# Two two-layer transformer models on one core: x in two feature halves, square roots on ScalarE, a held bank, and sums moved ahead

## The chip, the cores and the metric

One core of one Trainium2 chip runs the whole kernel in one launch. The metric is the time of the launch in device microseconds (us), the median of several runs.

## What is computed

One sequence of 512 tokens with 1024 features passes through two models in a row, each with two layers, all in float32. A layer of the first model projects x with `w_in`, runs four groups of attention (softmax with a forget gate; latent attention "mla"; stick breaking; a sliding window with sinks), normalises each group, multiplies by `w_o`, adds 1.414 x and applies a layer norm (ln1), then a gated MLP with a second layer norm (ln2). Cut to what matters here:

```python
for l in range(DEPTH):
    h = x @ w_in[l]
    (..., cq, ckv, kr, ..., wq, wk, wv) = jnp.split(h, points, axis=-1)
    out_b = _mla(cq, ckv, kr, ...)          # rms norms of cq and ckv, then products
    ...
    x = _layernorm(ALPHA * x + y, ln1_g[l], ln1_b[l])
    f = (silu(x @ w_gate[l]) * (x @ w_up[l])) @ w_down[l]
    x = _layernorm(ALPHA * x + f, ln2_g[l], ln2_b[l])
```

A layer of the second model has an MLP, a mixer (differential attention of 4 heads, a short convolution, a linear recurrence) and another MLP, each behind an rms norm; a last rms norm gives the output.

## The kernel before, in words

x is kept transposed in SBUF: 8 tiles X of 128 features by 512 tokens, with its two-part split XH (rounded to fp32r) and XL (the rest). A weight chunk is loaded by SP (`raw`, 3 buffers, L176), cast to `whi` by ScalarE (L181) and subtracted to `wlo` by VectorE (L186), four buffers each. A product is three matmuls, hi by hi, lo by hi and hi by lo (`mm3`, L196 to L198), on 512 tokens, or on half of them (256) where `half_units` and `halves` do one token half after the other, so that one half's vector work lies beside the other's products.

PE's order is written by hand: the order of the program. Work that needs an answer from another engine is put in a list of due times (`later`, a time in us) and each product counts its own time off (`tick`: 0.648 for 512 tokens, 0.327 for 256); what is due is issued between two products. `flush` issues all that is left. Products sum in eight PSUM banks: four of `mm`, which `in_turn` hands out in rotation, passing over banks in `held`; two of `sc`; `pt` and `pv`. In layer2's attention two of the four go over to `sc` (`more_scores`). VectorE's and ScalarE's orders come from a planner, by priority, except where `manual_schedule` keeps the order of the program: at the start of the first layer, and from `w_o`'s last products to the first MLP unit (ln1).

**Start (layer1, l = 0).** Tiles 0 and 1 of x (128 tokens by 1024 features each) are loaded whole, 0 by ScalarE's queue and 1 by SP's (L249); `wake` runs 11 products of zeros (L257); `turn_x` transposes 16 blocks (L266) into four banks, and its `parts` split them to XH and XL (L273, L274). Four chunks of `w_in` (two 128-feature rows each) follow on SP; each is cast in four pieces into the weights of two units, `chq` (L808, L809) and `chm` (L813 to L817). `half_units` then runs both units on the first token half (bank name `hg`). After 4.0 us of counted products `second_half` transposes tiles 2 and 3.

**lat_norm.** Squares of the latent values, sums by PE (`st`), `ve` (L853), then `rsqrt` on VectorE: a first guess by a shift and three Newton steps, 11 small operations (L222 to L228). `bc` (due at 5.2 and 5.9) transposes the result into a bank (L233) and the latent values are scaled.

**wkv and the latent products.** `wkv_evac` empties its bank by four copies, ScalarE and VectorE in turn (L987, L988). Then `g_mla_w` makes four latent values (`mv`, L950), each in a bank of `mm`, and `g_mla_qk(0)` takes two more (`uq`, `uk`).

**ln1 (Norm1 with pace).** `bank` adds a finished bank to X (L422), squares it (L424) and lets GpSimd add it to SA (L426). `half` adds the squares to SQ (L434), due at 3.6, or 5.6 for the second half, sums SA and SQ by PE (L333), finds mean and 1/sigma, and 3.8 later `bc` broadcasts them (L233). `tile_` normalises a tile (L459 to L464). In the first half the eight tiles are spread over the products of the second, and what is left is flushed at the end of them, ahead of `half`.

**layer2's head 0.** Ten counted us after a head's attention, `fn` transposes its 512 by 128 result into `pt` (L1644) and `split_scaled` reads it (L212, L213). Beside the steps of attention a `Fill` runs units of 16 products (`u`) from the two banks of `mm`.

**final_tail.** The last down product runs in two token halves. `consume` adds the bank to X, squares (L1390), applies the gain (L1374), transposes features 0 to 3 (L1378, `fin`); `stats` sums SQ and the squares (L1399), makes `ve` (L1401) and `rsqrt`, transposes features 4 to 7 and scales to the output (L1408, L1409, L1411).

Of the kernel before, what the change touches and what calls it, by code (L numbers as in the profile page):

```python
# [10 lines left out]
F32 = mybir.dt.float32  # L11
# [7 lines left out]
P = 128  # L19
S = 512  # L20
D = 1024
# [58 lines left out]
def model_kernel(ctx: ExitStack, tc: tile.TileContext, A: dict, out: bass.AP, n1=DEPTH, n2=DEPTH):  # L80
# [23 lines left out]
    last = [0]  # L104
# [125 lines left out]

    def bcast(dst, col):

        T.transpose(dst, col.to_broadcast([P, P]), ident)  # L233
# [14 lines left out]
    def load_x(xin, j):  # L248
        (nc.scalar if j in (0, 2) else nc.sync).dma_start(xin[j], A["x"][0, j * P:(j + 1) * P, :])  # L249

    def wake():
# [4 lines left out]
        for i in range(11):  # L256
            T.matmul(ps, z[:, :P], z, start=True, stop=True)  # L257

    def turn_x(xin, hh):
        hs = slice(hh * HALF, (hh + 1) * HALF)  # L260
        xps = []
        for t in range(0, ND, 2):
            ps = (mmt("xT") if t < 4 else sct("xT")).rearrange("p (m s) -> p m s", m=2)
            for m in range(2):
                for b in range(2):
                    T.transpose(ps[:, m, b * P:(b + 1) * P],  # L266
                                xin[2 * hh + b][:, (t + m) * P:(t + m + 1) * P], ident)
            xps.append((t, ps))
# [13 lines left out]
        parts.copies = copies  # L282
# [83 lines left out]
    class Norm1:  # L366
# [50 lines left out]
        def bank(self, hh, t0, bank):  # L417
# [9 lines left out]
            self.sqs.append(s)  # L427

        def half(self, hh, banks):
# [5 lines left out]
            self.sqs = []  # L435

            def stats():
# [48 lines left out]
                later(3.8, bc)  # L486
            later(5.6 if self.pace and hh else 3.6, stats)
# [88 lines left out]
    def g_chunks(ch, evac, ncol=256, bank=mmt):  # L576
        for m in range(ncol // P):
# [3 lines left out]
            for k in range(ND):  # L581
                wh, wl = ch[k // 4]
                mm3(ps, wh[:, k % 4, c], wl[:, k % 4, c], XH[:, k], XL[:, k], k == 0, k == ND - 1, MF)
                if k == ND - 1:
                    let_go("unit")
                    evac(m, ps)
# [158 lines left out]
    def layer1(l):  # L745
        w_in = A["w_in"][l]
        with tc.tile_pool(name="at1", bufs=1) as ap_:
# [39 lines left out]
            chq, chm = [], []  # L787
            if l == 0:
                splits = turn_x(xin, 0)
# [5 lines left out]
            for k0 in range(0, ND, 2):  # L795
                rf = wchunk(w_in, k0 * P, 2, 768, 420, split=False)
                if l == 0 and k0 == 2:
                    load_x(xin, 2)
                if l == 0 and k0 == 4:
                    load_x(xin, 3)  # L800
                if l == 0 and k0 < 4:
                    splits(2)
                if k0 % 4 == 0:
                    chq.append(wsplit(4, 256))
                    chm.append(wsplit(4, 256))
                ks = slice(k0 % 4, k0 % 4 + 2)
                hi, lo = [t[:, ks] for t in chq[-1]]
                SC.copy(hi, rf[:, :, 4:260])  # L808
                V.tensor_sub(lo, rf[:, :, 4:260], hi.bitcast(F32))  # L809
                hi, lo = [t[:, ks] for t in chm[-1]]  # L810
# [7 lines left out]
                if l == 0 and k0 == 4:  # L818
                    splits.copies()
            if l == 0:  # L820
# [3 lines left out]
                later(4.0, second_half)  # L824
# [15 lines left out]
            def lat_norm():  # L840
# [6 lines left out]
                def stats():  # L847
# [18 lines left out]
                    later(5.2, lambda: bc((2,), 0))  # L866
                    later(5.9, lambda: bc((0, 1), NB))
# [116 lines left out]
            def wkv_evac(m, ps):  # L984
                if m == 0:
                    for kv in range(2):
# [221 lines left out]
            drain(gw)  # L1208
            drain(g_mla_qk(0))
# [140 lines left out]
    def layer2(l):  # L1350
# [19 lines left out]
        def final_tail(down, nkt, hview):  # L1370
# [10 lines left out]

            def consume(hh, banks):
# [9 lines left out]
                got = {(j, 0): turn(sct("fin"), j, 0) for j in js}  # L1392

                def stats():
                    st = pvt("st")
                    for a, j in enumerate(js):
                        for i, src in enumerate((SQ[:, j * P:(j + 1) * P], s[:, 0, a * P:(a + 1) * P],
                                                 s[:, 1, a * P:(a + 1) * P])):
                            T.matmul(st[:, a:a + 1], src, mcol, start=(i == 0), stop=(i == 2))  # L1399
# [383 lines left out]
```

## Time and profile before

| | |
|---|---|
| runs | 3172.09 us median of 3 (3172.02 to 3172.25) |
| profiled execution | 3171.67 us, its span 3169.9 us |
| TensorE busy | 3136.2 us, 99% of the span |
| weight loads, VectorE, ScalarE, GpSimd | 84%, 51%, 37%, 4% |
| granted TensorE clock, mean | 0.998 |

Times in the rows count from the start of the span. PE is TensorE, DVE VectorE, ACT ScalarE, POOL GpSimd; SPq and ACTq are the queues that issue transfers. A row of a timeline gives start, duration, engine, line, operation, what it writes and reads, how many follow each other, and in brackets how long the engine sat idle before it and what ended that. Matmuls overlap, so the duration of one is longer than its distance to the next.

### The profile page before, as it was taken

Reading aid. Unit: us, or ns where it says so; the run is one execution under the profiler, and the core shown is the slowest. Engines: PE = TensorE matmul, PEld = TensorE weight load, DVE = VectorE, ACT = ScalarE, POOL = GpSimd, SP = SyncE. Lnnn points to the kernel's source line nnn. Section 1 sums busy time; section 2 is a strip of 40 time slices with the busy share of each in tenths; the row PEclk is TensorE's granted clock in tenths of the full one; section 3 lists DMA queues with packets and bytes.
Section 4 is the critical chain, followed back from the end, with each engine's and each line's share of the span. In section 5 each row is a group of like instructions: output and inputs, shape, how many; then the busy total and the mean of one; then the engine's idle time right before and its main releaser. Section 6 shows DMA issues by size and latency. Waiting matters only on the chain.

```text
span 3169.9 us, 40582 instructions
## 1 busy us (share of the span) xinstructions
PE 3136.2 (99%) x16387; PEld 2651.4 (84%) x16387; DVE 1602.9 (51%) x2849; ACT 1164.8 (37%) x1989; POOL 127.6 (4%) x168
## 2 busy tenths in 40 slices
PE   8999999999999999999999999999999999999999
PEld 7889888988888889988888888888888888788888
DVE  6566333575763334844336764443544336754433
ACT  5454322264543222523223543232323224443322
POOL 1002000020020000000000000000000000000000
PEclk9999999999999999999999999999999999999999
DMA  4121333341203333433333223333333332133322
GB/s 144 44 68 54 97 94 97 115 124 40 78 28 107 100 95 110 123 100 93 98 98 97 71 81 100 100 93 100 95 99 93 97 108 88 57 100 100 93 95 85
DMA packets 283822, 289.97 MB, mean 91 GB/s; under 512 B 10261, under 2 KB 280161, under 8 KB 283633
## 3 DMA queue, kind: packets, MB, share of 16 engines
q1 hardware_dynamic: 280752, 282.73, 29.7%
q0 software_dynamic: 2304, 3.07, 0.5%
q8 instruction: 128, 2.10, 0.3%
q10 hardware_dynamic: 576, 1.57, 0.1%
q14 instruction: 62, 0.50, 0.0%
HBM read 285.22 MB, written 2.11 MB: 91 GB/s over the span
## 4 chain that ended last, share of the span: by engine, by line
PE 92%; DVE 4%; ACT 2%; issue 1%; POOL 1%; DMA 0%; DVEq 0%; ACTq 0%; POOLq 0%; SPq 0%
PE u L196 18%; PE u L197 17%; PE u L198 17%; PE o L196 7%; PE o L197 7%; PE o L198 7%; PE pv L724 2%; PE oh L196 2%; PE oh L197 2%; PE oh L198 2%; PE pt L717 1%; PE ut L598 1%; PE ut L600 1%; PE ut L599 1%; PE sc L1053 1%; PE hg L197 1%
## 5 line engine op out<-in xcount | busy, mean ns | idle before, releaser
L186 DVE TENSOR_TENSOR wlo<-raw,whi 128x1024 fp32r<-128x1024 f32 (+2 forms) x562 | 635.7, 1136 | 847.8 <-ACT whi L181 847.1
L196 PE MATMUL u<-XH,whi 128*128 128x512 f32 x2496 | 980.1, 393 | 0.0
L198 PE MATMUL u<-XH,wlo 128*128 128x512 f32 x2496 | 972.3, 390 | 0.0
L197 PE MATMUL u<-XL,whi 128*128 128x512 f32 x2496 | 971.7, 389 | 0.0
L181 ACT CAST whi<-raw 128x1024 fp32r<-128x1024 f32 (+1 forms) x526 | 540.4, 1028 | 945.0 <-PE o L197 407.8
L198 PEld LDWEIGHTS u<-XH,wlo 128*128 128x128 f32 x2496 | 468.6, 188 | 98.8
L196 PEld LDWEIGHTS u<-XH,whi 128*128 128x128 f32 x2496 | 468.9, 188 | 97.5 <-issue 2.2
L197 PEld LDWEIGHTS u<-XL,whi 128*128 128x128 f32 x2496 | 469.0, 188 | 93.8
L196 PE MATMUL o<-hh,whi 128*128 128x512 f32 x836 | 325.6, 389 | 0.0
L198 PE MATMUL o<-hh,wlo 128*128 128x512 f32 x836 | 325.3, 389 | 0.0
L197 PE MATMUL o<-hl,whi 128*128 128x512 f32 x836 | 325.2, 389 | 0.0
L656 ACT ACTIVATE gs<-gs 128x512 f32<-128x512 f32 x88 | 55.5, 632 | 407.4 <-DVE gs L654 407.2
L198 PEld LDWEIGHTS o<-hh,wlo 128*128 128x128 f32 x836 | 156.9, 188 | 32.6
L197 PEld LDWEIGHTS o<-hl,whi 128*128 128x128 f32 x836 | 157.0, 188 | 32.6
L196 PEld LDWEIGHTS o<-hh,whi 128*128 128x128 f32 x836 | 157.0, 188 | 32.3
L655 DVE TENSOR_TENSOR us<-u,SA 128x512 f32<-128x512 f32 x86 | 59.5, 692 | 165.5 <-PE u L198 165.5
L196 PE MATMUL oh<-hh,whi 128*128 128x256 f32 x440 | 125.0, 284 | 0.0
L198 PE MATMUL oh<-hh,wlo 128*128 128x256 f32 x440 | 124.5, 283 | 0.0
L197 PE MATMUL oh<-hl,whi 128*128 128x256 f32 x440 | 124.5, 283 | 0.0
L654 DVE TENSOR_TENSOR gs<-u,SA 128x512 f32<-128x512 f32 x86 | 58.9, 685 | 89.2 <-PE u L198 89.2
L197 PEld LDWEIGHTS oh<-hl,whi 128*128 128x128 f32 x440 | 84.4, 192 | 0.1
L196 PEld LDWEIGHTS oh<-hh,whi 128*128 128x128 f32 x440 | 84.4, 192 | 0.1
(401 smaller groups left out, 3883.6 us busy)
## 6 DMA issues: line engine op xcount, KB each, us to landing
raw<-ffn_gate SPq DMA_DIRECT2D x88, 512.0 KB, 3.7
raw<-ffn_up SPq DMA_DIRECT2D x88, 512.0 KB, 3.7
raw<-ffn_down SPq DMA_DIRECT2D x82, 512.0 KB, 3.4
raw<-w_in SPq DMA_DIRECT2D x76, 512.0 KB, 3.8
raw<-w_down SPq DMA_DIRECT2D x54, 512.0 KB, 3.4
raw<-w_gate SPq DMA_DIRECT2D x44, 512.0 KB, 3.7
raw<-w_up SPq DMA_DIRECT2D x44, 512.0 KB, 3.7
raw<-w_o SPq DMA_DIRECT2D x16, 512.0 KB, 3.5
```

Of the source, the lines that this page charges most:

```text
L181: SC.copy(hv, rv)
L186: V.tensor_sub(lv[:, ks], rv[:, ks], hv[:, ks].bitcast(F32))
L196: T.matmul(ps, wh, xh, start=start, stop=False)
L197: T.matmul(ps, wh, xl, start=False, stop=False)
L198: T.matmul(ps, wl, xh, start=False, stop=stop)
L598: T.matmul(ps, XH[:, k, js], wh[:, k % 4], start=(k == 0), stop=False)
L599: T.matmul(ps, XH[:, k, js], wl[:, k % 4], start=False, stop=False)
L600: T.matmul(ps, XL[:, k, js], wh[:, k % 4], start=False, stop=(k == ND - 1))
L654: V.tensor_mul(v(gs), v(g), bcv)
L655: V.tensor_mul(v(us), v(u), bcv)
L656: SC.activation(gs, gs, AF.Silu)
L724: T.matmul(self.pv_out(), self.pts[:, a * P:(a + 1) * P], self.vfn(j), start=(a == 0), stop=(a == len(self.kb) - 1))
```

## The change

x's first two tiles arrive in two pieces of 512 features; wake-up is 8 products. Chunk 0 of the weights is asked for behind the first pieces, and only features 0 to 511 are turned ahead of the first products; features 512 to 1023, chunks 4 and 6 and the second token half come at 2.4, 4.4 and 6.4 us of counted products. The four weight buffers are taken as chq, chq, chm, chm in both layers. `lat_norm` and `final_tail` use ScalarE's Sqrt, VectorE's reciprocal and one Newton step. ln1's squares are added between tiles, and its due times change. The wkv bank is held until the four latent values are made. Head 0's result goes to a bank of `mm`. In `final_tail` the transposes and SQ's sums of the second token half move among its products. Cut to its core:

```diff
+    def between(n, fn):
+        n = min(n, len(pend))
+        pend.insert(n, [pend[n - 1][0] if n else 0.0, fn])
+    def rsqrt_by_root(ve, n):
+        y = sp.tile([P, 8], F32, tag="ry", name="ry")[:, :n]
+        q = sp.tile([P, 8], F32, tag="rq", name="rq")[:, :n]
+        SC.activation(q, ve, AF.Sqrt)
+        V.reciprocal(y, q)
+        V.scalar_tensor_tensor(q, y, -0.5, ve, op0=ALU.mult, op1=ALU.mult)
+        V.tensor_mul(q, q, y)
+        V.scalar_tensor_tensor(y, q, 1.5, y, op0=ALU.add, op1=ALU.mult)
+        return y
-        for i in range(11):
+        for i in range(8):
             T.matmul(ps, z[:, :P], z, start=True, stop=True)
...
@@ Norm1.bank, Norm1.half @@
             self.sqs.append(s)
+            if self.pace and hh:
+                between(3 if len(self.sqs) == 2 else 2, lambda: self.add_squares(hh))
...
-                later(3.8, bc)
-            later(5.6 if self.pace and hh else 3.6, stats)
+                later(4.0 if self.pace and hh else 3.8, bc)
+            later(4.2 if self.pace and hh else 3.6, stats)
...
@@ layer1, start @@
-                load_x(xin, 0)
-                load_x(xin, 1)
+                for j in range(2):
+                    load_x(xin, j, 0, D // 2)
                 wake()
+            chq = [wsplit(4, 256) for _ in range(2)]
+            chm = [wsplit(4, 256) for _ in range(2)]
...
+                fetch(0)
+                for j in range(2):
+                    load_x(xin, j, D // 2, D // 2)
+                fetch(2)
+                splits = turn_x(xin, 0, ND // 2)
+                splits(1)
+                weights(0, lambda: splits(1))
+                def stage2():
+                    load_x(xin, 2)
+                    fetch(4)
+                    load_x(xin, 3)
+                    weights(2)
+                    splits.turn(range(ND // 2, ND, 2))
+                    splits(2)
+                    fetch(6)
+                def stage4():
+                    weights(4)
                     splits.copies()
+                    weights(6)
-                later(4.0, second_half)
+                later(2.4, stage2)
+                later(4.4, stage4)
+                later(6.4, second_half)
...
@@ lat_norm @@
-                        r = rsqrt(ve, 2 * NB)
+                        r = rsqrt_by_root(ve, 2 * NB)
-                    later(5.2, lambda: bc((2,), 0))
-                    later(5.9, lambda: bc((0, 1), NB))
+                    later(5.6, lambda: bc((2,), 0))
+                    later(6.3, lambda: bc((0, 1), NB))
...
@@ wkv_evac (m == 0), and behind the latent values @@
+                    held["kv"] = unit[0]
...
             drain(gw)
+            let_go("kv")
             drain(g_mla_qk(0))
...
@@ final_tail @@
+            def ahead(hh):
+                js = (2 * hh, 2 * hh + 1)
+                got = {(j, 0): turn(sct("fin"), j, 0) for j in js}
+                st = pvt("st")
+                for a, j in enumerate(js):
+                    T.matmul(st[:, a:a + 1], SQ[:, j * P:(j + 1) * P], mcol, start=(a == 0), stop=False)
+                ahead.of = got, st
...
-                    r = rsqrt(ve[:, :2], 2)
+                    r = rsqrt_by_root(ve[:, :2], 2)
...
+                    if hh == 0:
+                        later(6.0, lambda: ahead(1))
...
+            SC.activation(root[:, :1], mcol, AF.Sqrt)
             out_halves(down, nkt, hview, consume, (3,))
...
@@ layer2, fn of a head's end @@
-                                ps = ptt()
+                                ps = ptt() if h else mmt()
```

`weights(k0, between)` holds the casts and subtracts of one chunk, as before, and runs `between` behind the first cast and subtract. `add_squares` is the loop over L434.

## Rows read from the trace of the kernel before

**Rows 1.** Page, part 1: busy us, share of the span, instructions.

```profile
PE 3136.2 (99%) x16387; PEld 2651.4 (84%) x16387; DVE 1602.9 (51%) x2849; ACT 1164.8 (37%) x1989; POOL 127.6 (4%) x168
```

**Rows 2.** PE's waits over the span: us in total, times, longest us.

```profile
PE mv L950 <- DVE wqk L988: 4.0, 2, 2.1
PE pt L717 <- DVE YL L213: 3.0, 2, 1.5
PE hg L196 <- ACT XH L463: 2.8, 2, 1.4
PE st L333 <- DVE SQ L434: 2.0, 3, 0.7
PE xT L266 <- DMA O<-x: 0.3, 1, 0.3
```

**Rows 3.** Timeline of the start.

```profile
1.28 4.47 PE L257 MATMUL wake<-zeros 128*128 128x512 bf16 x11 [1.28 <-DVE zeros L254]
...
8.98 0.62 ACT L808 CAST whi<-raw 128x512 fp32r<-128x512 f32 x1 [1.68 <-DMA raw<-w_in]
...
9.65 0.38 PE L196 MATMUL hg<-XH,whi 128*128 128x256 f32 x1 [2.15 <-ACT whi L808]
```

**Rows 4.** Windows of the start: us, engines' busy us, then PEclk, DMA share, GB/s.

```profile
0.00:5.00 5.00, 3.72 (x9) 1.34 (x10) 0.39 (x4) 1.28 (x1) 3.95 (x12) 1.00 0.66 222
5.00:6.00 1.00, 1.00 (x7) 0.70 (x6) 0.00 (x0) 0.00 (x0) 0.47 (x1) 1.00 0.89 9
6.00:9.00 3.00, 1.50 (x14) 1.26 (x12) 1.29 (x2) 1.09 (x3) 0.90 (x2) 1.00 0.94 222
9.00:12.00 3.00, 2.12 (x15) 1.92 (x16) 2.37 (x7) 3.00 (x9) 1.35 (x4) 1.00 1.06 401
```

**Rows 5.** Timeline of the latent norm, first layer.

```profile
45.03 0.17 DVE L853 TENSOR_SCALAR ve<-st 128x8 f32<-128x8 f32 x1 [1.06 <-PE st L333]
...
46.07 1.28 ACT L1322 ACT_TABLE_LOAD   x1
...
47.37 0.20 ACT L1322 ACTIVATE e<-e 128x4 f32<-128x4 f32 x1
...
52.59 1.06 PE L233 MATMUL sc<-ident,ry 128*128 128x128 f32 x8 [1.30 <-DVE fb L772]
```

**Rows 6.** Timeline of the latent norm, second layer.

```profile
692.00 0.17 DVE L228 SCALAR_TENSOR_TENSOR ry<-rq,ry 128x8 f32<-128x8 f32 x1
...
694.93 1.03 PE L233 MATMUL sc<-ident,ry 128*128 128x128 f32 x8
```

**Rows 7.** VectorE's second copy out of wkv's bank, first layer.

```profile
60.15 0.69 DVE L988 COPY wqk<-u 64x512 f32<-64x512 f32 x1
```

**Rows 8.** Timelines of VectorE and PE in ln1, first layer.

```profile
278.54 0.42 DVE L459 TENSOR_TENSOR nw<-X,sc 128x256 f32<-128x256 f32 x1 [1.35 <-PE sc L233]
...
285.95 3.03 DVE L434 TENSOR_TENSOR SQ<-SQ,sq 128x256 f32<-128x256 f32 x4
...
296.57 0.39 PE L196 MATMUL hg<-XH,pre 128*128 128x256 f32 x1 [1.40 <-ACT XH L463]
```

**Rows 9.** Windows behind ln1's wait; columns as in rows 4.

```profile
299.00:302.00 3.00, 3.00 (x16) 3.00 (x15) 1.88 (x5) 2.92 (x7) 2.37 (x4) 0.50 0.00 0
303.00:306.00 3.00, 3.00 (x27) 3.00 (x26) 0.82 (x2) 2.96 (x7) 1.47 (x2) 1.00 0.00 0
```

**Rows 10.** Timeline behind head 0 of layer2, first layer.

```profile
1803.13 0.39 PE L196 MATMUL u<-XH,whi 128*128 128x512 f32 x1
...
1803.36 0.68 DVE L1551 TENSOR_TENSOR ysc<-ysc,u 128x512 f32<-128x512 f32 x1
```

**Rows 11.** Timeline of the tail.

```profile
3159.33 1.04 PE L1378 MATMUL fin<-ident,X 128*128 128x128 f32 x8
...
3160.64 0.89 ACT L1374 ACTIVATE X<-X,vc 128x256 f32<-128x256 f32 x2
...
3164.23 1.41 DVE L1408 TENSOR_SCALAR fo<-fin,ry 128x512 f32<-128x512 f32 x2
```

More of the change, by code (lines that the diff above doesn't have):

```diff
@@ L103, in in_turn @@
         return t
-    last = [0]
+    last, unit = [0], [0]
     def hold(key):
@@ L281, in copies @@
                 SC.copy(X[:, t:t + 2, hs], ps)
-        parts.copies = copies
+        parts.copies, parts.turn = copies, turn
         parts.done = 0
@@ L427, in bank, with add_squares @@
             self.sqs.append(s)
-        def half(self, hh, banks):
+            if self.pace and hh:
+                between(3 if len(self.sqs) == 2 else 2, lambda: self.add_squares(hh))
+        def add_squares(self, hh):
             hs = slice(hh * HALF, (hh + 1) * HALF)
@@ L435, in half @@
             self.sqs = []
+        def half(self, hh, banks):
+            hs = slice(hh * HALF, (hh + 1) * HALF)
+            self.add_squares(hh)
             def stats():
@@ L584, in g_chunks @@
                 if k == ND - 1:
+                    unit[0] = held["unit"]
                     let_go("unit")
@@ L794, in layer1, with weights @@
                    (slice(176, 192), slice(388, 404)))
[L795 to L805, printed above, removed]
+            def weights(k0, between=None):
+                rf = raws.pop(k0)
                 ks = slice(k0 % 4, k0 % 4 + 2)
-                hi, lo = [t[:, ks] for t in chq[-1]]
+                hi, lo = [t[:, ks] for t in chq[k0 // 4]]
                 SC.copy(hi, rf[:, :, 4:260])
                 V.tensor_sub(lo, rf[:, :, 4:260], hi.bitcast(F32))
-                hi, lo = [t[:, ks] for t in chm[-1]]
+                if between is not None:
+                    between()
+                hi, lo = [t[:, ks] for t in chm[k0 // 4]]
                 gsrc = rf[:, :, 0:4].unsqueeze(2).to_broadcast([P, 2, 16, 4])
@@ L823, in second_half @@
                     splits(4, False)
-                later(4.0, second_half)
+                later(2.4, stage2)
+                later(4.4, stage4)
+                later(6.4, second_half)
+            else:
+                for k0 in range(0, ND, 2):
+                    fetch(k0)
+                    weights(k0)
             lat = [ap_.tile([P, 544], F32, tag=tg, name="lat")[:, :S] for tg in ("om", "cp", "wv")]
@@ L1391, in consume @@
                 gain((6, 7), hs)
-                got = {(j, 0): turn(sct("fin"), j, 0) for j in js}
+                if hh == 0:
+                    ahead(hh)
+                got, st = ahead.of
                 def stats():
[L1395 to L1399, printed above, removed]
+                    for m in range(2):
+                        for a in range(2):
+                            T.matmul(st[:, a:a + 1], s[:, m, a * P:(a + 1) * P], mcol, start=False, stop=(m + a == 2))
                     ve = sp.tile([P, NB], F32, tag="ve", name="ve")
                     V.tensor_scalar(ve[:, :2], st[:, :2], 1e-6, None, op0=ALU.add)
-                    r = rsqrt(ve[:, :2], 2)
+                    r = rsqrt_by_root(ve[:, :2], 2)
                     got[js[0], 1] = turn(ptt(), js[0], 4)
@@ L1416, in final_tail @@
             gain(range(6), slice(0, S))
+            root = sp.tile([P, 8], F32, tag="rhv", name="root")
+            SC.activation(root[:, :1], mcol, AF.Sqrt)
             out_halves(down, nkt, hview, consume, (3,))
```

32 lines of the change are left out of this document (17 added, 15 removed).

## The prediction, made before the change was run

> **What bounds the kernel now.** I read the page's busy times first: TensorE is busy 3136.2 us of a span of 3169.9 [rows 1], so another engine counts only where it makes PE wait, and a change can win little more than the 34 us in which PE stands idle, unless products run slower somewhere. The next view is therefore the list of PE's waits [rows 2]. The change touches its largest entries: the latent values that wait for a bank (4.0 us in two waits), the transposes behind head 0 of layer2 (3.0), and ln1's second half (2.8 for XH, and two of the three waits for SQ; the third belongs to ln2). Timelines of these places come next, and of the start (2.15 us) [rows 3] and the latent norm (1.30) [rows 5]. Last comes the granted clock: behind ln1's waits it reads 0.50 in a stretch where PE is never idle [rows 9]. A list of waits doesn't show that loss.
>
> The profiled execution took 3171.67 us; the median of the runs is 0.42 above it. The sum goes against 3171.67, and 0.42 is added at the end.
>
> A group of three 256-column products takes about 0.36 us: 27 products in 3 us, those cut by the edges counted [rows 9].
>
> **Start.** Wake-up products run from 1.28 to 5.75. ScalarE's cast of weight chunk 0 starts when the chunk lands, at 8.98, and the first product follows 0.67 later, at 9.65, after 2.15 us of idle [rows 3]. By 5.0 us 1.11 MB have moved (the identity and two x tiles); from 5 to 6 the queues are busy but move 9 GB/s, then 222 GB/s [rows 4]. After, chunk 0 needs the identity, two half tiles and itself (0.43 MB) and, if ScalarE's queue goes on beside it, the other half of tile 0: 1.28 MB instead of 1.54. At 6.0 some 0.16 MB are left, 0.7 us: 6.7. The same reckoning gives 7.9 for before, where 8.98 was seen; I take 7.0, near the reckoning, and the first product at 7.7. The bounds are 5.5 (ScalarE's half waits, and the chunk passes the hole) and 8.98 (the transfers in the hole set the landing, not the bytes). Of the 1.95 won, 0.95 goes back: eight of the sixteen transposes move behind the first products (the tail's eight take 1.04 with their last drain [rows 11]). The splitting of x that now stands between chunk 0's casts, a cast like the 0.62 of rows 3 and a subtract, makes the second unit's weights later: 0.5 more. The 0.3 that PE waited for x's second token half [rows 2] is covered, since its transfer moves ahead less than PE gives back. Net **0.8 won** (bounds 1.2 lost, 2.3 won). Three wake-up products fewer cost nothing while x is awaited. Later chunks and x's third tile, whose issue stands behind chunk 0's casts on ScalarE, have at least PE's eight transposes more time; if they are late, that is the lower bound.
>
> The Trainium skill (DMA: Bandwidth & Descriptors, Queues, rings and completion order) has each DMA engine serve its queues in turn, packet by packet. By that rule the half tile on ScalarE's queue does run beside chunk 0, as in the sum; without it the sum would be some 0.7 better. No row separates the two.
>
> **Latent norm (both layers).** Eleven small VectorE operations become a root on ScalarE and four. In the first layer ve is ready at 45.2; PE reaches the broadcast at 51.29 and waits 1.30 [rows 5]. After: a table load of 1.28, a root of 0.2, and four operations of 0.17, for which I allow 0.9 each with what stands between them: 50.3, so the wait goes. In the second layer ry is ready at 692.17 and PE comes at 694.93 [rows 6]: another load makes it 1 to 2 us later, inside the 2.76 in hand. Nothing lost, bound 1.0. The load is paid beside products. **1.3 won** (bounds 1.0 lost, 1.3 won).
>
> The Trainium skill speaks against it (ScalarE: Activation LUTs, What ACT_TABLE_LOAD costs, and Table sets: the hidden batching unit): group calls by table set; a change of set costs 2.66 us, a drain included. The row shows 1.28, with the next function 0.02 behind it, and no drain [rows 5]. By the page's price for the two changes, there and back, the first layer would still gain, but the second could lose up to 1.4: the sum would be up to 1.4 worse.
>
> **The held bank (both layers).** The fourth latent product waits until VectorE's second copy out of wkv's bank ends, at 60.84 [rows 7]. After, it takes another bank and runs at once. But the hold ends right behind it, the wkv bank is then the oldest in the rotation, and uq's first product takes it, with the same wait. Only the fourth product's 0.36 moves ahead: **0.7 won** in two layers, of 4.0 (bounds 0 and 4.0).
>
> **ln1's second half (both layers).** By counted product time 18 groups stand before the statistics and 12 more before the broadcast; after, 13 and 13. The broadcast moves ahead by four groups, 1.4 us, and the wait of 1.40 for XH [rows 8] goes but for some 0.15. The 0.7 for SQ goes too: its four adds, 3.03 us at the end of VectorE's list for the first half [rows 8], move up between tiles. What is late instead is the first half. The first bank's two adds (0.76 each) now stand ahead of tile 0, for which VectorE had idled 1.35 us [rows 8]. If they fit into that idle time, tile 0 is 0.2 late; if their square comes last, 1.5. I take 0.75, halfway, and PE passes it on, since it takes tile 0 at once. Per layer 0.7 + 1.4 - 0.15 - 0.75 = 1.2, **2.4 won** in all (bounds 0 and 4.0). GpSimd's sums lie beside it as before.
>
> **The clock behind it.** Behind the XH wait PE runs at 0.50, which is 1.2 GHz, in all of the 3 us shown, 16 products against 27 at 1.00 (2.4 GHz) [rows 9]. So some 11 products' time is lost, 1.2 us, and with the stretch's ends 1.5 per layer; the second layer repeats the wait [rows 2]. After, 0.15 is left there, and 0.75 stands alone far ahead. **3.0 won** (bounds 0 and 3.0; the start's 2.15 us left the clock at 1.00 [rows 4], so the length of a wait alone doesn't decide).
>
> **Head 0 of layer2 (both layers).** The transposes go to a main bank, and the 1.5 us of waiting for YL's read go. But there are two such banks, and taking one turns the rotation: the next unit's first product, at 1803.13, gets the bank that VectorE reads from 1803.36 to 1804.04 [rows 10], not the free one. It waits 0.95: **1.1 won** in all (bounds 0 and 3.0).
>
> **Tail.** Eight transposes and two sums of SQ move ahead of the last products, which end 1.1 later. Before, the outputs' scaling starts at 3164.23, 4.9 after the last product made way at 3159.33 [rows 11]. After, ScalarE's gains end 2.2 behind the last product [rows 11], then a root of 0.25, four operations of 0.2 and 0.1 of handover: 3.35. Won 4.9 - 3.35 - 1.1, about **0.4** (bounds 0.6 lost, 1.5 won). The table load that prepares it lies beside some 30 us of products.
>
> The second layer's first weight buffers are taken in another order; the list of waits has none there, so I count nothing (bound 1.0 lost).
>
> **Sum.** 0.8 + 1.3 + 0.7 + 2.4 + 3.0 + 1.1 + 0.4 = 9.7. 3171.67 - 9.7 + 0.42 = **3162.4**. 0.2% is 6.3 us, about what a measurement of this kernel can tell from no change: faster means below 3165.7, slower above 3178.4.
>
> **Rivals.** (a) *The halved x brings nothing forward.* The hole sets chunk 0's landing, and PE, warmed by eight products instead of eleven, has one stretch at 0.50. For it: 9 GB/s in the hole; against: the clock stood 2.15 us of idle. The start loses 1.2 and 1.5: 3165.9. Chance 0.16. (b) *ln1's waits move but stay as long*, and 0.50 with them: 5.4 less won, 3167.8. For it: VectorE pays the 3.03 us for SQ wherever it stands. Chance 0.2. (c) *The bank waits go altogether*, because the banks are emptied sooner than I read: 3.3 and 1.9 more, 3157.2. Chance 0.08. (d) *Slower*: the adds ahead of tile 0 hold ln1's first half 1.9 us per layer, 0.50 follows there, and the second half keeps its waits and its 0.50: 6.9 not won, 2.3 and 3.0 paid, 3174.6. It decides from a hold of about 1 us upward, if the second half's waits stay. Against it: the 1.35 us of idle ahead of tile 0. Chance 0.06. (e) The page's price for the tables: 3163.8. Chance 0.02, since the row has no drain. The forecast keeps 0.48, its own range 3160 to 3165.
>
> **Numbers.** Below 3165.7 lie nearly all of the forecast, half of (a), a fifth of (b), all of (c) and (e): faster 0.68. Same, 0.29: the rest of these and (d). Slower, 0.03: costs not seen here. The range reaches to (a) and (b) and leaves out (d) and most of (c): 3158.8 to 3167.8.
>
> **What would show it.** Right: a first product near 7.7; no wait for ry; a wait of 1.7 us at uq instead of at the latent values; about 0.75 at the first half of ln1, at most 0.3 for XH in its second, no 0.50; about 0.95 at the unit behind head 0. A first product at 9 or later, 0.50 behind ln1, or over 1 us for a root makes the prediction wrong.

## The result, and the profile after

The changed kernel takes 3219.53 us (median of 4, 3218.28 to 3223.41) against 3172.06 before: a ratio of 1.0152 (95% 1.014 to 1.0165). It is 47 us slower, where 9.7 us less was forecast, and it lies far outside the range. The profiled execution took 3218.28 us, its span is 3216.5.

The page's part 1 is the first place to look:

```profile
PE 3188.3 (99%) x16384; PEld 2653.2 (82%) x16384; DVE 1601.2 (50%) x2817; ACT 1169.7 (36%) x1998; POOL 124.5 (4%) x168
```

PE's idle time is the span less its busy time: 28.2 us after, 33.7 before [rows 1]. The waits have shrunk. What has grown is PE's busy time, by 52.1 us, with three products fewer. PE's waits after confirm it: some are new, but the longest entry is 3.6 us in all, far from 47 (columns as in rows 2):

```profile
PE uq L201 <- DVE wqk L1041: 3.6, 2, 1.9
...
PE u L201 <- DVE ysc L1618: 1.6, 2, 0.8
PE hg L201 <- ACT whi L830: 1.5, 1, 1.5
PE hg L201 <- ACT lat L886: 1.4, 1, 1.4
...
PE st L1462 <- ACT sq L1453: 1.0, 1, 1.0
```

So the products themselves must be slower, and the view that shows it is the groups by line with the shapes kept apart (count, busy us, mean ns of one). First the kernel before, whose rows of this view are not shown ahead:

```profile
L196 PE MATMUL u<-XH,whi 128*128 128x512 f32 x2496 | 980.1, 393 | 0.0
L198 PE MATMUL u<-XH,wlo 128*128 128x512 f32 x2496 | 972.3, 390 | 0.0
L197 PE MATMUL u<-XL,whi 128*128 128x512 f32 x2496 | 971.7, 389 | 0.0
L196 PE MATMUL o<-hh,whi 128*128 128x512 f32 x836 | 325.6, 389 | 0.0
...
L196 PE MATMUL oh<-hh,whi 128*128 128x256 f32 x440 | 125.0, 284 | 0.0
```

The same groups after:

```profile
L201 PE MATMUL u<-XH,whi 128*128 128x512 f32 x2496 | 992.9, 398 | 1.6 <-DVE ysc L1618 1.6
L203 PE MATMUL u<-XH,wlo 128*128 128x512 f32 x2496 | 985.0, 395 | 0.0
L202 PE MATMUL u<-XL,whi 128*128 128x512 f32 x2496 | 984.6, 394 | 0.0
L201 PE MATMUL o<-hh,whi 128*128 128x512 f32 x836 | 330.1, 395 | 0.0
...
L201 PE MATMUL oh<-hh,whi 128*128 128x256 f32 x440 | 124.6, 283 | 0.0
```

Every 512-column group on the split weights (`whi`, `wlo`) has the same count and is 3 to 6 ns longer by its mean; the 256-column group is not. Groups of 512 columns on other weights keep theirs: uk on kvhl, 394 before and 395 after, or bd, 592 in both. The mean hides the pace, since products overlap. A window of 100 us in the first MLP, where PE never idles, gives it: before, then after (columns as in rows 4).

```profile
1000.00:1100.00 100.00, 100.00 (x443) 82.84 (x442) 32.89 (x35) 28.93 (x36) 0.00 (x0) 1.00 0.34 100
```

```profile
1000.00:1100.00 100.00, 100.00 (x432) 81.08 (x431) 33.15 (x35) 28.56 (x36) 0.00 (x0) 1.00 0.33 95
```

443 products against 432, both at a granted clock of 1.00 (2.4 GHz), with the other engines as busy as before: 2.5% more for each product. The timeline after shows the form of it (start, duration; out and in tiles):

```profile
999.65 0.39 PE L202 MATMUL u<-XL,whi 128*128 128x512 f32 x1
999.89 0.39 PE L203 MATMUL u<-XH,wlo 128*128 128x512 f32 x1
1000.12 0.39 PE L201 MATMUL u<-XH,whi 128*128 128x512 f32 x1
1000.35 0.39 PE L202 MATMUL u<-XL,whi 128*128 128x512 f32 x1
1000.58 0.40 PE L203 MATMUL u<-XH,wlo 128*128 128x512 f32 x1
1000.81 0.40 PE L201 MATMUL u<-XH,whi 128*128 128x512 f32 x1
1001.05 0.40 PE L202 MATMUL u<-XL,whi 128*128 128x512 f32 x1
1001.28 0.39 PE L203 MATMUL u<-XH,wlo 128*128 128x512 f32 x1
1001.51 0.39 PE L201 MATMUL u<-XH,whi 128*128 128x512 f32 x1
```

From the start at 1000.12 to the one six products later, at 1001.51, are 1.39 us; before, six products take 1.36 (1000.13 to 1001.49). No product waits for anything that the trace lists. A loss that is spread so evenly over all 512-column products isn't a matter of the places that the change touches. It is something that holds for the whole program.

Between the two programs three things hold throughout. The split weight tiles lie elsewhere: a pool lays its tiles out in the order in which each kind is first asked for. The change asks for split tiles ahead of the first raw chunk, so whi and wlo begin 73344 and 89728 bytes into the partition, where raw began; before, they began at 86016 and 102400, behind raw. X, XH, XL, HH, HL, YH and YL have kept their addresses. Then, the PSUM banks rotate in another order. Last, the start is another one, if some state of TensorE lasted from there.

### The profile page after: what moved, and what is told of

It is laid out like the page before. It is cut to its first block, busy times and chain, and to the rows that moved or that the text cites. A ratio compares the mean times of both kernels' runs of the same rounds, so it can differ in the third digit from the quotient of the medians.

```text
span 3216.5 us, 40550 instructions
## 1 busy us (share of the span) xinstructions
PE 3188.3 (99%) x16384; PEld 2653.2 (82%) x16384; DVE 1601.2 (50%) x2817; ACT 1169.7 (36%) x1998; POOL 124.5 (4%) x168
## 4 chain that ended last, share of the span: by engine, by line
PE 92%; DVE 4%; ACT 2%; issue 0%; DMA 0%; POOL 0%; DVEq 0%; ACTq 0%; POOLq 0%; SPq 0%
PE u L201 18%; PE u L203 18%; PE u L202 18%; PE o L201 7%; PE o L202 7%; PE o L203 7%; PE pv L750 2%; PE oh L201 1%; PE oh L202 1%; PE oh L203 1%; PE pt L743 1%; PE hg L202 1%; PE hg L201 1%; PE hg L203 1%; PE sc L1106 1%; PE ut L624 1%
## 5 line engine op out<-in xcount | busy, mean ns | idle before, releaser
L201 PE MATMUL u<-XH,whi 128*128 128x512 f32 x2496 | 992.9, 398 | 1.6 <-DVE ysc L1618 1.6
L203 PE MATMUL u<-XH,wlo 128*128 128x512 f32 x2496 | 985.0, 395 | 0.0
L202 PE MATMUL u<-XL,whi 128*128 128x512 f32 x2496 | 984.6, 394 | 0.0
```

Of the source, the lines that this page charges most:

```text
L201: T.matmul(ps, wh, xh, start=start, stop=False)
L202: T.matmul(ps, wh, xl, start=False, stop=False)
L203: T.matmul(ps, wl, xh, start=False, stop=stop)
```

## The experiments

### Moving the weights back, and moving them in the kernel before

Four kernels ran on one chip, with the kernel before beside them at 3171.99 us (median of 25). In each no instruction differs from the kernel that it is made from; only addresses do.

The changed kernel, with a pool of its own for raw, ahead of the split tiles:

```
+    rp = ctx.enter_context(tc.tile_pool(name="rp", bufs=1))
     wp = ctx.enter_context(tc.tile_pool(name="wp", bufs=1))
-        raw = wp.tile([P, 1056], F32, tag="raw", bufs=3, name="raw")
+        raw = rp.tile([P, 1056], F32, tag="raw", bufs=3, name="raw")
```

> The changed kernel with every instruction as it stands; only the raw weight tiles get a pool of their own that is laid out ahead of the split ones, so that the split weight tiles whi and wlo lie where they lay before (86016 and 102400 bytes into the partition; in the changed kernel, which asks for a split tile first, 73344 and 89728). Theory of the place (the 512-column products are slower because the weights lie elsewhere): the 512-column rows go from 395 ns back to 389 ns, PE's busy time loses the some 52 us that it gained, and the time is about 3166 us (3163 to 3169), below the kernel before, since the idle time of 28.3 us stays. Theory of the banks (the other rotation of PSUM banks slows the products): place changes nothing, 3219 us. Theory of the start (the other first 10 us put TensorE into a slower pace that lasts): 3219 us.

Measured: 3165.15 us (3164.29 to 3169.35), ratio to before 0.9981 (0.9971 to 0.999). PE is busy 54.0 us less, and the u rows are those of before:

```profile
PE 3134.3 (99%) x16384; PEld 2648.9 (84%) x16384; DVE 1601.0 (51%) x2817; ACT 1169.5 (37%) x1998; POOL 124.6 (4%) x168
...
L202 PE MATMUL u<-XH,whi 128*128 128x512 f32 x2496 | 980.4, 393 | 1.6 <-DVE ysc L1619 1.6
```

The kernel before, with that pool declared behind the split tiles:

```
     wp = ctx.enter_context(tc.tile_pool(name="wp", bufs=1))
+    rp = ctx.enter_context(tc.tile_pool(name="rp", bufs=1))
-        raw = wp.tile([P, 1056], F32, tag="raw", bufs=3, name="raw")
+        raw = rp.tile([P, 1056], F32, tag="raw", bufs=3, name="raw")
```

> The kernel before with every instruction as it stands; only the raw weight tiles get a pool of their own behind the split ones, so that whi and wlo lie where the changed kernel has them (73344 and 89728). Theory of the place: the 512-column rows go from 389 to 395 ns and the time is about 3226 us (3220 to 3230), slower than the changed kernel by the idle time that the change did remove. Theory of the banks, and theory of the start: 3172 us, since banks and start are those of before.

Measured: 3227.79 us, ratio 1.0175 (1.0159 to 1.019), with the long rows:

```profile
L197 PE MATMUL u<-XH,whi 128*128 128x512 f32 x2496 | 993.0, 398 | 0.0
```

So the place of the weights is worth 54.4 us in the one kernel and 55.8 in the other. Banks and start are ruled out: each stayed as it was while the time went. Two more kernels ask what about the place matters. The first puts the split tiles at 73728, by padding:

```
+    z1 = ctx.enter_context(tc.tile_pool(name="z1", bufs=1))
     wp = ctx.enter_context(tc.tile_pool(name="wp", bufs=1))
+    rp = ctx.enter_context(tc.tile_pool(name="rp", bufs=1))
-        raw = wp.tile([P, 1056], F32, tag="raw", bufs=3, name="raw")
+        raw = rp.tile([P, 1024], F32, tag="raw", bufs=3, name="raw")
+    z1.tile([P, 96], F32, name="pad1")
```

> The changed kernel with 384 bytes of padding ahead of the split weights and raw tiles that much narrower: whi at 73728, wlo at 90112, again multiples of 4096 bytes, but not where they lay before; all else in its place. Theory of the place, alignment variant (what counts is where the tile starts within a power of two): as fast as with the raw tiles first, 3166 us. Theory of the place, distance variant (what counts is which tiles lie there, or how far from XH): still 3219 us or between. Banks or start: 3219 us.

Measured: 3166.94 us, ratio 0.9983 (0.9974 to 0.9993), u rows at 393 ns: fast. What lies there and the full distance from XH don't matter; the offset in some power of two does.

The second sets that offset to 256 bytes:

```
+    rp = ctx.enter_context(tc.tile_pool(name="rp", bufs=1))
+    z1 = ctx.enter_context(tc.tile_pool(name="z1", bufs=1))
     wp = ctx.enter_context(tc.tile_pool(name="wp", bufs=1))
+    z2 = ctx.enter_context(tc.tile_pool(name="z2", bufs=1))
-        raw = wp.tile([P, 1056], F32, tag="raw", bufs=3, name="raw")
+        raw = rp.tile([P, 1024], F32, tag="raw", bufs=3, name="raw")
+    z1.tile([P, 32], F32, name="pad1")
+    z2.tile([P, 64], F32, name="pad2")
```

> The changed kernel with the raw tiles first, 128 bytes narrower each, and a padding that puts whi at 85760 and wlo at 102144: 256 bytes past a multiple of 512, 128 and 0 being the places of the changed kernel and of before. Theory of the place: fast (3166 us) if 256 bytes of alignment are enough, slow (3219 us) if it takes 512, and a third pace if the cost grows with the offset. Banks or start: 3219 us.

Measured: 3167.29 us, ratio 0.9986 (0.9977 to 0.9996), u rows at 393 ns: fast. A multiple of 256 is enough; 512 isn't needed.

### Weights alone, or weights against the moving tile

XH, XL, HH and HL all lie on multiples of 256, so the runs so far can't say whether the weights have to lie on such a multiple or on the same offset as the tile that moves past them. The kernel before, with XH and the weights both 128 bytes further, and HH and HL not:

```
-    gp.tile([P, 96], F32, name="lead")
-    sp.tile([P, 40], F32, name="foot", bufs=1)
+    gp.tile([P, 128], F32, name="lead")
+    sp.tile([P, 8], F32, name="foot", bufs=1)
```

> The kernel before with the padding ahead of the stream's tiles 128 bytes longer and the padding ahead of the MLP's tiles as much shorter: X, XH, XL and the split weights all lie 128 bytes further (128 past a multiple of 256), HH, HL, YH and YL where they were (on one). No instruction differs. If what counts is the distance of the weights from the moving tile (both on the same offset is fast): the u rows stay at 389 ns, the o rows from HH and HL go to 395 ns, about 3187 us (836 x 3 rows x 5.5 ns more). If the place of the weights alone counts: both at 395 ns, about 3227 us. If either operand off a multiple of 256 is enough: the same 3227 us.

Measured in a single run: 3187.97 us, against 3170.47 before on this chip. The rows come apart just so, u short and o long:

```profile
L196 PE MATMUL u<-XH,whi 128*128 128x512 f32 x2496 | 980.5, 393 | 0.0
...
L196 PE MATMUL o<-hh,whi 128*128 128x512 f32 x836 | 330.5, 395 | 0.0
```

The kernel before, with XH 128 bytes further and the weights on a multiple of 256:

```
-    gp.tile([P, 96], F32, name="lead")
-    sp.tile([P, 40], F32, name="foot", bufs=1)
+    gp.tile([P, 128], F32, name="lead")
+    sp.tile([P, 104], F32, name="foot", bufs=1)
-        raw = wp.tile([P, 1056], F32, tag="raw", bufs=3, name="raw")
+        raw = wp.tile([P, 1024], F32, tag="raw", bufs=3, name="raw")
```

> The kernel before with X, XH and XL 128 bytes further and the split weights still on a multiple of 256 (the raw tiles are narrower), HH and HL where they were. Distance between the operands: the u rows go to 395 ns, the o rows from HH stay at 389 ns, about 3211 us (2496 x 3 rows x 5.2 ns more). Place of the weights alone: nothing changes, 3172 us. Either operand off a multiple of 256: as by the distance, 3211 us; this case and the run beside it together tell the three apart.

Measured in a single run: 3210.34 us, and the rows are the other way round:

```profile
L196 PE MATMUL u<-XH,whi 128*128 128x512 f32 x2496 | 992.8, 398 | 0.0
...
L196 PE MATMUL o<-hh,whi 128*128 128x512 f32 x836 | 325.7, 390 | 0.0
```

The distance theory had said 3187 and 3211, and the others 3227 or 3172 in at least one of the two. It is the difference of the two operands' addresses, modulo 256 bytes, that sets the pace of these 512-column products: 0 is fast on 0 and 0, on 256 and 0, and on 128 and 128; 128 is slow whichever operand carries it. How the chip comes to this is open; the runs show only the pace.

A last offset, 64, with the pads of the earlier kernel at 48 and 48 elements:

```
-    z1.tile([P, 32], F32, name="pad1")
-    z2.tile([P, 64], F32, name="pad2")
+    z1.tile([P, 48], F32, name="pad1")
+    z2.tile([P, 48], F32, name="pad2")
```

> The changed kernel with the raw tiles first and the split weights 64 bytes past a multiple of 256 (0 was fast, 128 slow). If only a multiple of 256, or of 128 with something else, is fast: slow, 395 ns and about 3219 us. If the cost goes with the offset: a third pace between or beyond. If 64 happens to be harmless: 389 ns and about 3166 us.

Measured in a single run: 3223.57 us. The u rows are at 398 ns, as with 128, so the cost is not in proportion to the offset. The 256-column rows, however, get shorter with it:

```profile
L206 PE MATMUL u<-XH,whi 128*128 128x512 f32 x2496 | 993.3, 398 | 1.6 <-DVE ysc L1623 1.6
...
L206 PE MATMUL oh<-hh,whi 128*128 128x256 f32 x440 | 122.6, 279 | 0.0
```

### What the rest of the change is worth, on weights in their place

With the weights back the forecast's own steps can be read, as differences in when PE reaches the same instruction (start in us; the profile of the run with raw first against that of before):

| instruction | before | weights back | difference |
|---|---|---|---|
| first product | 9.65 | 8.86 | -0.8 |
| sums of the first latent norm (st) | 43.16 | 44.16 | +1.0 |
| first product of the latent values (mv) | 57.62 | 57.13 | -0.5 |
| first token-wise unit (ut) | 130.39 | 130.45 | +0.1 |
| sums of ln1's second half, first layer | 287.82 | 286.91 | -0.9 |
| sums in the down products behind ln1, first layer | 561.55 | 558.53 | -3.0 |
| sums of the second layer's latent norm | 686.97 | 683.17 | -3.8 |
| the second layer's first ut | 772.79 | 769.19 | -3.6 |
| the same sums, second layer | 1203.00 | 1196.33 | -6.7 |
| last sums ahead of the tail's products | 2799.54 | 2791.95 | -7.6 |
| end of span | 3169.9 | 3162.5 | -7.4 |

These are differences of two single executions, and small ones vary from one to the next. The start stands out: the first product comes 0.8 earlier, and by 43 us PE is 1.0 behind. Windows of the three us behind the first product: the run with the weights back, then the changed kernel itself.

```profile
9.00:12.00 3.00, 3.00 (x13) 2.77 (x14) 2.02 (x7) 1.82 (x7) 1.77 (x5) 0.50 1.07 402
```

```profile
9.00:12.00 3.00, 2.96 (x12) 2.74 (x13) 2.10 (x6) 1.29 (x6) 1.20 (x3) 1.00 1.03 384
```

The first has the granted clock at 0.50 (1.2 GHz) and 13 products. The second says 1.00 but has 12, and its products last 0.41 to 0.58 us each, those of the kernel before 0.28 to 0.39: the clock record of that trace starts only behind this window, and misses the fall. The rotation of banks stands out too: mv to ut loses 0.6. These two were mended in one kernel:

```
-        for i in range(8):
-            T.matmul(ps, z[:, :P], z, start=True, stop=True)
+
+        def more(n):
+            for i in range(n):
+                T.matmul(ps, z[:, :P], z, start=True, stop=True)
+        more(11)
+        return more
...
-                wake()
+                awake = wake()
...
                 splits = turn_x(xin, 0, ND // 2)
+                awake(6)
...
-            let_go("kv")
             drain(g_mla_qk(0))
+            let_go("kv")
```

> The changed kernel with the split weights back in their place, and two more edits. The wake products are 11 again and 6 more stand behind the first transposes, where TensorE waits 2.0 us for the first weights: if the idle time there is what lets the granted clock fall to 0.50 from 8.6 to 12.1 us, the stretch is gone and the first latent sums (st, at 44.2 us with the split weights back, 43.2 before) come 1.5 to 2 us earlier. And the bank that is kept for the copy of wk is given free behind the products of uq instead of ahead of them: if the wait of 1.7 to 2.0 us at uq in each layer is only that the rotation gives uq that very bank, it goes, 1.5 to 2 us in each layer; if uq needs the vector engine for something else there, it stays. Together 3160 us (3158 to 3163) by these reasons, 3165 us if neither holds.

Measured: 3160.23 us (3159.91 to 3161.73), ratio 0.9968 (0.9956 to 0.998). That is 4.9 below the run with the weights back, but on another chip, where the kernel before takes 3170.47; the two traces are 4.4 apart, 1.0 of it by the first sums and 1.4 and 2.0 between mv and ut of the two layers. Both reasons hold. The window has the clock at 1.00, and the first sums come at 43.19:

```profile
9.00:12.00 3.00, 2.75 (x21) 2.37 (x20) 1.75 (x6) 1.40 (x6) 1.54 (x4) 1.00 1.05 390
```

Of the idle times from 40 to 72 us, the run with the weights back has these two of over 0.2 us (the last bracket is the idle time and what ended it):

```profile
59.07 0.39 PE L1003 MATMUL mv<-kvhl,LH 128*128 128x256 f32 x1 [0.70 <-ACT mv__545 L1007]
61.40 0.47 PE L202 MATMUL uq<-LH,uhl 128*128 128x512 f32 x1 [1.71 <-DVE wqk L1042]
```

With the bank let go later, 0.72 at mv stays, uq's wait is gone, and 0.71 appears at the first scores:

```profile
58.12 0.39 PE L1008 MATMUL mv<-kvhl,LH 128*128 128x256 f32 x1 [0.72 <-ACT mv__554 L1012]
64.30 0.46 PE L1208 MATMUL sc<-KH,QH 96*128 96x128 f32 x2 [0.71 <-DVE QH L1027]
```

The mv wait is the price of a held bank: three banks for four products, and the fourth waits until ScalarE has copied the first.

That the fall at the start belongs to the shorter wake-up and the idle time behind it rests on more traces than these two. All five traced kernels with eight wake products go at the slow pace there, and none of the four with the filled-up start does; their first latent sums come at 44.16 to 45.45 and at 43.19 to 43.46 us. One kernel with eleven wake products and no more has a fall there too: the kernel before with the weights moved, where PE waits 2.77 us for the first weights.

Then each of four kernels undoes one part of the change on this base (3160.23 us). They ran on a third chip, where the kernel before takes 3170.83 us (3170.47 beside the base), and the 95% intervals of all five ratios overlap. So the differences are read from the traces as well as from the times. The start, with its edit cut to what PE sees (the wake products stay 11, without the 6; the order of the weight buffers and the due time of 4.0 go back too):

```
-                splits = turn_x(xin, 0, ND // 2)
-                awake(6)
+                splits = turn_x(xin, 0)
...
-                    load_x(xin, j, 0, D // 2)
+                load_x(xin, 0)
+                load_x(xin, 1)
```

> The kernel with the split weights in place, the bank of wk's copy freed later and the wake products filled up (3160.2 us), with one part of the change undone: x's first half arrives in one piece again, all 16 transposes and 11 wake products stand ahead of the first product, as in the kernel before. If the two parts of x bring what the prediction priced (0.8 us): the first latent sums come 0.8 us later and the time is 3161.0 us. If the halved transfer brings nothing forward once the clock stays up: first sums where they are, 43.2 us in both, and 3160.2 us. If the shorter order is what lets the clock fall: a gain here, 3159 us.

Measured: 3159.45 us (3159.42 to 3159.51), ratio 0.9965 (0.9952 to 0.9978): 0.8 below the base by the times, taken on another chip. In the traces the first sums come at 43.00 (43.19 in the base), both kernels reach the second layer's latent sums at 680.68, and their outputs' scaling starts at 3152.01 and 3152.07: the part is worth nothing. ScalarE's cast of chunk 0, in the changed kernel and in this one:

```profile
8.37 0.62 ACT L830 CAST whi<-raw 128x512 fp32r<-128x512 f32 x1 [1.11 <-DMA raw<-w_in]
```

```profile
8.28 0.62 ACT L835 CAST whi<-raw 128x512 fp32r<-128x512 f32 x1 [0.54 <-DMA raw<-w_in]
```

The chunk lands no earlier behind two halves than behind two whole tiles. This holds over all traces: the cast starts at 8.00 to 8.37 in the nine kernels with halves, and at 8.10, 8.16 and 8.28 in three of the five with whole tiles. The other two are 9.77 and the 8.98 of before, from which the prediction reckoned [rows 3]; so the 0.8 at the first product in the table is a late landing of that one execution, and not the change's work. Half a tile less ahead of the chunk brings nothing.

The tail:

```
-            def ahead(hh):
...
-                got, st = ahead.of
+                got = {(j, 0): turn(sct("fin"), j, 0) for j in js}
...
-                    r = rsqrt_by_root(ve[:, :2], 2)
+                    r = rsqrt(ve[:, :2], 2)
```

> The same base with the part behind the last products undone: transposes, sums and the vector engine's root as in the kernel before. The prediction gave the changed tail 0.4 us: then 3160.6 us here. The milestones of the run with the split weights back say that it costs some 0.2 us (the root saves about 1 us on the vector engine, the moved transposes and a wait of 1.0 us for the last square take as much): then 3160.0 us. Either is under what timing tells; the span behind the last 256-column product tells it: 9.3 us as changed, 10.4 us as before, with 8 transposes and 4 sums, some 1.2 us, more or less ahead of it.

Measured: 3160.4 us (3160.14 to 3162.08), which timing can't tell from the base. In the traces the outputs' scaling starts at 3152.07 with the changed tail and at 3152.60 without, of which 0.35 was there before the last half's products (PE reaches them 12.00 and 11.65 us ahead of the kernel before): 0.2 us is the tail's worth.

The squares:

```
-            if self.pace and hh:
-                between(3 if len(self.sqs) == 2 else 2, lambda: self.add_squares(hh))
...
-                later(4.0 if self.pace and hh else 3.8, bc)
-            later(4.2 if self.pace and hh else 3.6, stats)
+                later(3.8, bc)
+            later(5.6 if self.pace and hh else 3.6, stats)
```

> The same base with the squares summed where they were before, ahead of each second half's statistics, and the waits ahead of those statistics at their old length. By the prediction's terms (waits 2.4 us and granted clock 3.0 us over both layers): 3165.6 us, with stretches at a clock of 0.50 behind both first layer norms. By the milestones (3.1 us in each layer): 3166.3 us. If the clock behind ln1 falls for another reason, the waits come back alone: 3162.6 us.

Measured: 3163.43 us (3162.91 to 3166.39), 3.2 above the base, and 3.2 by the traces too (1.6 in each layer). The waits are back in their old length, and the clock stays up in the profiled execution:

```profile
PE hg L202 <- ACT XH L491: 2.8, 2, 1.4
...
PE st L357 <- DVE SQ L458: 1.8, 3, 0.7
```

```profile
299.00:302.00 3.00, 3.00 (x27) 3.00 (x26) 0.32 (x1) 2.97 (x6) 0.85 (x2) 1.00 0.01 3
```

So the wait for XH is not by itself what lets the granted clock fall behind ln1, as it does in the profile of before [rows 9]. The kernel before with the weights moved has the same wait, 1.40 up to 300.01 us, and no fall behind it either:

```profile
303.00:306.00 3.00, 3.00 (x27) 3.00 (x27) 1.32 (x4) 2.92 (x6) 2.09 (x3) 1.00 0.01 3
```

Falls come and go between executions. The kernel before and its three versions with other addresses have the waits in both layers, and a fall behind six of these eight. The wait at uq is followed by one in some executions and not in others. And the time goes with the clock: of 25 timed runs of the kernel before on one chip, the three with a mean granted clock of 0.999 take 3169.02 to 3169.92 us, the five with 0.997 take 3173.38 to 3175.3. Of the ten runs without the squares' part three have 0.998 and take 3164.86 us or more; all six of the base have 0.999. So the waits may make a fall more likely; that is not shown.

The latent norm's root:

```
-                        r = rsqrt_by_root(ve, 2 * NB)
+                        r = rsqrt(ve, 2 * NB)
...
-                    later(5.6, lambda: bc((2,), 0))
-                    later(6.3, lambda: bc((0, 1), NB))
+                    later(5.2, lambda: bc((2,), 0))
+                    later(5.9, lambda: bc((0, 1), NB))
```

> The same base with the latent norm's root by the vector engine again and its products due as before. By the prediction (one wait of 1.3 us in the first layer): 3161.5 us. By the milestones (1.5 us in the first layer, 0.8 in the second): 3162.5 us.

Measured: 3161.17 us (3160.8 to 3161.85), 0.9 above the base in times and traces, of which 0.3 stood already at the first sums. The wait for ry is back, but the one at mv goes:

```profile
52.90 1.06 PE L250 MATMUL sc<-ident,ry 128*128 128x128 f32 x8 [1.31 <-DVE fb L803]
...
65.13 0.46 PE L1208 MATMUL sc<-KH,QH 96*128 96x128 f32 x2 [0.64 <-DVE QH L1027]
```

PE, when late by 1.3, finds the latent values' banks copied. So the root is worth 1.3 where it stands and 0.6 at the end. In the second layer it is worth nothing: from 686.97 to 699.92 in the times of before, PE neither gains nor loses.

## Why the prediction was wrong

**The step that failed.** The change part by part went through instructions, queues, waits and banks. It did not ask where tiles lie, though the first lines of the new start ask for the split weights before any raw chunk, and the pool's layout follows from that. Of weights asked for in another order it said "so I count nothing (bound 1.0 lost)", for buffers and waits. The term that was left out measures 54.4 us, and no rival had it. The opening paragraph held the door open ("unless products run slower somewhere") and no step went through it. With the weights in their place the same instructions take 3165.15 us, inside the range, 2.8 above the forecast. That nearness is in part luck: the start and the held bank came out 3.3 worse than forecast, and ln1, with falls of the clock that come and go, and a wait that vanished by chance came out 1.6 better.

By the prediction's own signs, the wait at uq and the end of the waits for ry and XH came as told. Its sign "a first product at 9 or later" came too, 9.04 in the changed kernel.

**The steps that held, by the run with the weights back:**
- ln1's second half and the clock behind it. 5.4 us were forecast for both; PE gets 3.1 further ahead in each layer (from +0.1 to -3.0, and from -3.6 to -6.7, in the table). The waits alone are 3.2 by the run without the squares' part, where 2.4 stood, since tile 0's price was smaller than 0.75: the changed kernel's idle time is 0.42 there.

```profile
282.91 0.38 PE L202 MATMUL hg<-XL,pre 128*128 128x256 f32 x1 [0.42 <-POOL XL L489]
```

- The clock's 3.0 was of the right size for the profiled execution of before: 6.2 less the 3.2. But the prediction took the fall to be a part of the wait, and the run without the squares' part has the waits and no fall. What decides is open; the prediction itself had noted that the length of a wait alone doesn't.
- Latent norm: 1.3 forecast, and PE is 1.5 further there; a part of it is given back at mv. The steps of the sum held: a table load of 1.28 with the root 0.02 behind it, and ry ready 4.7 us behind ve where 5.1 was reckoned.

```profile
46.03 0.17 DVE L906 TENSOR_SCALAR ve<-st 128x8 f32<-128x8 f32 x1 [1.07 <-PE st L353]
...
47.07 1.28 ACT L241 ACT_TABLE_LOAD   x1
...
48.37 0.21 ACT L241 ACTIVATE rq<-ve 128x8 f32<-128x8 f32 x1
...
50.73 0.16 DVE L245 SCALAR_TENSOR_TENSOR ry<-rq,ry 128x8 f32<-128x8 f32 x1
...
52.12 0.60 PE L250 MATMUL sc<-ident,ry 128*128 128x128 f32 x4
```

  The rows say 1.28 with no drain behind it, and rival (e) is out. By the Trainium skill's price of 2.66 us with a drain (ScalarE: Activation LUTs, What ACT_TABLE_LOAD costs) ry would, as an estimate, have come at 52.3, with PE at the broadcast at 52.12.
- Head 0 of layer2: 1.1 forecast, 0.9 measured (two steps of 0.46 at the sums of 1872.02 and 2799.54 us); the new wait at the next unit was to be 0.95 and is 0.8.

**The steps that failed by their size:**
- Start: 0.8 was to be won, 1.0 is lost. The landing of chunk 0 was reckoned from the bytes ahead of it, 7.0; it is 8.0 to 8.4, as with whole tiles (8.10 to 8.28 in three of five traces). Rival (a) had both halves of this, a landing that the bytes don't set and a stretch at 0.50 behind fewer wake products; that the hole sets it was not tested. The half-clock stretch is what loses the time, since filling the idle time gave the 1.0 back.
- The held bank: 0.7 was to be won, 0.8 is lost. The wait at uq came where and as long as foretold, 1.7. The wait at mv for the three banks that were left, 0.7, was not in the sum.
- Tail: 0.4 forecast, 0.2 by the run without it. The profile has PE idle 1.0 for the last square, which had stood behind the eight transposes.
- Not foreseen: 0.8 between the down products behind ln1 and the second layer's latent norm. Before, PE waits 0.42 us for XL at 679.40. The other order of buffers is not the cause: two kernels with the new order have this wait and take 125.3 and 125.5 us there, as before (125.4), and the version with x whole, in the old order, has none and takes 124.7, as do both versions of the kernel before with XH moved. The wait comes and goes between executions.

## What to carry to other kernels

When PE's busy time changes and its count doesn't, leave the waits alone and compare the mean of the same group in both traces; then compare tile addresses in both programs, since a request that moves ahead of another can move every tile of the pool. For products of two fp32r operands with 512 columns, as here, keep the weights and the moving tile on the same offset modulo 256 bytes, and give tiles that must stay so a pool, or padding, of their own, so that an edit elsewhere can't move them. A version with the weights in place, the bank let go later, full wake products and x whole takes 3159.45 us, 0.35% below the kernel before, and beats both kernels.

## What the runs showed that was not expected

- The offset between weights and moving tile costs 2.5% of a 512-column product (432 against 443 in 100 us) at an unchanged granted clock, and nothing in the list of waits shows it. With 256 columns a product is not slower but shorter: 284 ns on the same offset, 283 at 128, 279 at 64. Since the mean hides the pace, the windows from 1255 to 1275 us, which hold 256-column products alone in the three kernels, say more: 169, 171 and 179 products. Why 512 columns lose and 256 don't is open; offsets of 32 or 192 were not tried.
- A granted clock of 1.00 in a window is no proof: the changed kernel's 12 products from 9 to 12 us went at the pace of the 13 at 0.50 in another run, in a stretch that its clock record doesn't reach.
- Two executions of the same instructions can differ by a landing (8.10 to 9.77 us for the same first chunk), by a wait (0.42 for XL) and by falls of the clock. A term read from one trace holds only as far as a second trace repeats it.
